# Dense matmuls between the passes of a block inverse, and the order of three groups of loads in the third quarter, in a one-core hybrid RWKV-7 and sparse-attention layer

## The chip, the cores and the metric

The kernel runs on one core of a Trainium2 chip. The metric is the device time of one execution in microseconds (us); less is better. The kernel before takes 1706.21 us, the median of three runs between 1706.05 and 1706.52.

## The reference

One decoder layer in float32 on 1024 tokens of width 1024. A normalized input is projected once by `w_in`. Its parts feed RWKV-7 time mixing (8 heads of 64) and sparse attention, in which an indexer picks 256 keys for each query. Both are projected back, gated channel by channel and merged, and a SwiGLU network follows:

```python
u = rmsnorm(h, norm1_g)
proj = u @ w_in
y_a = rwkv7_mix(token_shift(p_rwkv, tshift_mu), ...)
y_b = dsa_attention(q, k, v, q_idx, k_idx, w_idx)
g_a, g_b = jnp.split(jax.nn.sigmoid(p_gate), 2, axis=-1)
merged = g_a * (y_a @ w_o_rwkv) + g_b * (y_b @ w_o_att)
h = h + merged @ w_out
z_gate, z_up = jnp.split(rmsnorm(h, norm2_g) @ w_ffn_in, 2, axis=-1)
h = h + (jax.nn.silu(z_gate) * z_up) @ w_ffn_out
```

The time mixing is a recurrence over tokens on a state of 64x64 for each head:

```python
sa = einsum('bhij,bhj->bhi', state, -kk_t)
state = state * d_t + sa * (kk_t * a_t) + v_t * k_t
y_t = einsum('bhij,bhj->bhi', state, r_t)
```

To it comes a bonus: the sum of r, k and r_k over a head, times v.

## The kernel before

**Dense work as filling.** The tokens are worked in two halves of 512. Every large product (projections, merge, feed-forward) splits weights and activations into a high and a low part and sums three matmuls of 128x512 for each block of 128 rows (`mm3`, L137: L142 and L143 for the high weights, L147 for the low ones; `mm3_last` with L160 likewise). These products, and attention, are generators in a queue `fill`. `pump(n)` (L177) takes n matmuls' worth from it, and `ticks(n, m)` takes n in m portions. The recurrence calls them between its steps, so dense matmuls fill TensorE while other engines work on a step. TensorE's order is just the order of the calls (it is scheduled by hand); ScalarE (ACT), VectorE (DVE), GpSimd (POOL) and SyncE (SP) get theirs from a scheduler, which places each instruction by its model of when its inputs are there.

**The recurrence.** `rwkv(half, ...)` (L548) runs two quarters of 256 tokens, q = 0 to 3 in all. A quarter's tokens form chunks of 64, each with a triangular system that is solved through the inverses of its two 32x32 blocks. In one quarter, in this order:

- The inputs are loaded, and the sums of the bonus go to memory (`d_bs`, L695). In the third quarter (q = 2) the merge of the first half is put into the queue here (`ready`, `settled`): from then on its products are what fills TensorE.
- Masked products of keys and queries, `MT`, are made by TensorE (L710) and VectorE (L714). Their 32x32 diagonal blocks, the mask blocks, go to memory in eight stores (`d_n`, L721) and come back with matrices along partitions in two loads (`N`, L742).
- VectorE inverts them by forward substitution: 31 steps of two operations (L751 and L753), the first of 128x31, at most of 128x136.
- The inverses go to memory (`d_w`, L755) and come back as blocks (`TT`, L764), which VectorE transposes into `TZ` (L767).
- The bonus sums are loaded, copied over 64 partitions (`bsp`, tile P, L771), and GpSimd multiplies `v` by them (L774).
- `ticks` (L775) then takes dense work from the queue.
- The block inverse: two passes (`pr`), each with 16 tiny 32x32 matmul pairs on `TZ` (L781) and two copies of the result back into `TZ` by ScalarE (L784). Then `inner(0)` (L787, its matmuls L791), a `pump(4)`, tiny matmuls that read those copies (L802), copies into `TT` (L805), and the steps over the chunks (from L843).

**The merge.** `merge(half)` (L1274) makes for each of eight blocks `d` of 128 channels two products in accumulators `acc` of PSUM, of which there are three buffers. `gates(d)` (L1280) loads the two gates into `tmp` tiles (four buffers, shared with attention) through SyncE's queue. VectorE multiplies a product with its gate (L1303, and L1305 or L1309 for the second), adds the two (L1310), ScalarE makes the high part (L1311) and VectorE the low part (L1312). The weights are converted by ScalarE (L116, `whi`) and VectorE (L117, `wlo`), two buffers of each.

`issue_after(x)` is a helper of the scheduler: what is issued inside it stands behind x in the order.

Of the kernel before, what the change touches and what calls it, by code (L numbers as in the profile page):

```python
# [51 lines left out]
def block_kernel(ctx: ExitStack, tc: tile.TileContext, ins: dict, outT: bass.AP, outR: bass.AP, stop=None, dbg=None):  # L52
    nc = tc.nc
    V, A, G, T, SY = nc.vector, nc.scalar, nc.gpsimd, nc.tensor, nc.sync
# [31 lines left out]
    def scratch(name, shape):  # L86
        return [dp.tile(shape, F32, name=f"{name}{h}") for h in range(2)]
# [8 lines left out]
    d_g = scratch("d_g", [16, 128, HT])  # L96
# [4 lines left out]
    d_bs = [dp.tile([2, 4, 256], F32, name=f"d_bs{q}") for q in range(4)]  # L101
    d_n = [dp.tile([64, 32, 32], F32, name=f"d_n{q}") for q in range(4)]
# [3 lines left out]
    def acc():  # L106
        return psA.tile([128, HT], F32, tag="acc", name="acc")

    def mix():
        return psM.tile([128, HT], F32, tag="mix", name="mix")  # L110

    def tmp():
        return tp.tile([128, HT], F32, tag="tmp", name="tmp")
# [63 lines left out]
    def pump(n):  # L177

        credit[0] += n
        while credit[0] > 0 and fill:  # L180
            try:
                credit[0] -= abs(next(fill[0]))
            except StopIteration:
                fill.popleft()
        if not fill:
            credit[0] = 0
# [3 lines left out]
    def ticks(n, m):  # L190

        for i in range(m):
            pump(n * (i + 1) // m - n * i // m)
            next(beside[0], None)
# [331 lines left out]
    def rwkv_consts(p):  # L526
# [18 lines left out]
        p.tile([128, 64], F32, name="edge")  # L545
        return cmask, wup, gup, rmask, ind, ind16

    def rwkv(half, p, consts, ready=None, settled=None):  # L548
        cmask, wup, gup, rmask, ind, ind16 = consts

        def t4(tag, shape=(128, 4, 256)):
            return p.tile(list(shape), F32, tag=tag, name=tag)

        for q in range(2 * half, 2 * half + 2):
# [184 lines left out]

            N = p.tile([128, 32, 32], F32, tag="x6", name="N")  # L740
            for par_ in range(2):
                SY.dma_start(N[64 * par_:64 * par_ + 64], d_n[q])  # L742
            W = p.tile([128, 16, 32], F32, tag="x7", name="W")
            V.memset(W, 0.0)
            for par_ in range(2):
# [22 lines left out]

            bsp = t4("P")
            for e in range(2):  # L770
                SY.dma_start(bsp[64 * e:64 * e + 64].rearrange("p c t -> p (c t)"),  # L771
                             d_bs[q][e].rearrange("c s -> (c s)").partition_broadcast(64))
            bon = v
            G.tensor_tensor(bon, v, bsp, op=ALU.mult)  # L774
            ticks((209, 231, 281, 232)[q], (13, 4, 10, 6)[q])  # L775
            both = [(h, pa, 64 - 64 * pa, 64 * pa) for h in range(8) for pa in range(2)]
            hd = [(h, h // 2, slice((h % 2) * 64, (h % 2) * 64 + 64), slice(h * 64, h * 64 + 64)) for h in range(8)]
            for pr in range(2):
                ps = mix()
                for h, pa, ba, kb in both:  # L780
                    T.matmul(ps[ba + 32:ba + 64, h * 32:(h + 1) * 32], MT[2 * pr + pa][ba:ba + 32, h, ba + 32:ba + 64],  # L781
                             TZ[ba:ba + 32, 0, pr, h, :], start=True, stop=True)
                for ba in (64, 0):
                    A.activation(TZ[ba + 32:ba + 64, 1, pr, :, :],  # L784
                                 ps[ba + 32:ba + 64, 0:256].rearrange("p (h t) -> p h t", h=8), AF.Copy)

            def inner(pr):  # L787
                ps = mix()
# [44 lines left out]
            for pr in range(2):  # L833
                yb = p.tile([128, 2, 512], F32, tag=("P", "x6")[pr], name="yb")
                yc, y2 = yb[:, 0, :], yb[:, 1, :]
                for pa in range(2):
                    c = 2 * pr + pa
# [436 lines left out]
    def merge(half, zp, zs):  # L1274
        yt = yhi, ylo = act_tiles(zp, "y", ("s0", "s1"))
        mt = act_tiles(zp, "m", ("s2", "s3"))
        for j in range(8):
            SY.dma_start(ylo[:, j, :].bitcast(F32), (d_ya if j < 4 else d_yb)[half][j % 4])

        def gates(d):  # L1280
            ga, gb = tmp(), tmp()
            SY.dma_start(ga, d_g[half][d])
            SY.dma_start(gb, d_g[half][8 + d])
            return ga, gb

        first_gates = gates(0) if half == 0 else None
        yield 0
        for j in range(8):
            split(yhi[:, j, :], ylo[:, j, :], ylo[:, j, :].bitcast(F32))
        yield -30  # L1290
        ahead = [weights(ins["w_o"][d]) for d in range(2)] if half == 0 else []
        for d in range(8):
            w = ahead[d] if d < len(ahead) else weights(ins["w_o"][d])
            ga, gb = first_gates if half == d == 0 else gates(d)
            pa = acc()
            pb = None
            if half == d == 0:
                pb = acc()
                yield from mm3_two((pa, pb), w, yt)
            else:  # L1300
                yield from mm3(pa, w, yt, nk=4)
            with tc.high_priority() if pb else nullcontext():
                V.scalar_tensor_tensor(ga, ga, 1.0, pa, op0=ALU.add, op1=ALU.mult)  # L1303
                if pb:
                    V.scalar_tensor_tensor(gb, gb, 1.0, pb, op0=ALU.add, op1=ALU.mult)  # L1305
            if pb is None:
                pb = acc()
                yield from mm3(pb, w, yt, nk=4, wk=4, ak=4)
                V.scalar_tensor_tensor(gb, gb, 1.0, pb, op0=ALU.add, op1=ALU.mult)  # L1309
            V.tensor_tensor(ga, ga, gb, op=ALU.add)  # L1310
            A.activation(mt[0][:, d, :], ga, AF.Copy, scale=0.5)  # L1311
            V.scalar_tensor_tensor(mt[1][:, d, :], ga, 0.5, mt[0][:, d, :].bitcast(F32), op0=ALU.mult,  # L1312
                                   op1=ALU.subtract)
        yield -10
        h = zp.tile([128, 8, HT], F32, tag="s0", name="h")
        load_x(half, h, range(8))
        sq = Rms(h)
        zt = zhi, zlo = act_tiles(zp, "z", ("s1", "s3")) if half == 0 else (None, None)
        pss = []
        if half == 0:  # L1320
            pss = [acc(), acc()]
            yield from mm3_last(pss, [weights(ins["w_out"][d]) for d in range(2)], mt, 8)
        for d in range(8):
            if d < len(pss):
                ps = pss[d]
            else:
                ps = acc()
                yield from mm3(ps, weights(ins["w_out"][d]), mt)
            V.tensor_tensor(h[:, d, :], h[:, d, :], ps, op=ALU.add)
            if half == 0:  # L1330
                A.activation(zhi[:, d, :], h[:, d, :], AF.Copy, scale=par[:, P_N2 + d:P_N2 + d + 1])
            SY.dma_start(d_h[half][d], h[:, d, :])
            sq.add(d)
        if half == 1:
            zs.append(sq)
            return
        for d in range(8):
            V.scalar_tensor_tensor(zlo[:, d, :], h[:, d, :], par[:, P_N2 + d:P_N2 + d + 1],
                                   zhi[:, d, :].bitcast(F32), op0=ALU.mult, op1=ALU.subtract)
        zs.extend((zt, sq))  # L1340
# [548 lines left out]
```

## Time and profile before

| what | us |
|---|---|
| median of three runs | 1706.21 |
| the profiled execution | 1709.14 |
| its span on the core | 1707.2 |
| TensorE busy | 1686.1 (99%) |
| VectorE busy | 1180.9 (69%) |
| ScalarE busy | 896.4 (53%) |
| GpSimd busy | 97.3 (6%) |

The profiled execution is one more run with the recorder on; the lines quoted below are of it, and the times in them are microseconds from the start of the span. In a line of the timeline stand the start, the duration, the engine, the source line, the operation, the tile written and the tiles read, the shapes and the count; a bracket at the end gives the idle time ahead of it on its engine and the instruction that ended it. A window's line gives its length, each engine's busy time, and at the end the granted TensorE clock (1.00 is full speed), the DMA engines' busy share and GB/s.

### The profile page before, as it was taken

To read this page: it belongs to the slowest core of one execution; us is meant where nothing else is said; L and a number is where in the kernel's file an instruction comes from. 1 tells how busy PE (TensorE), PEld (TensorE's weight loads), DVE (VectorE), ACT (ScalarE), POOL (GpSimd) and SP (SyncE) were. 2 spreads that over 40 slices of the span, in tenths; PEclk is the share of its full clock that TensorE was granted. 3 is DMA by queue.
4 is the path that set the end of the run, shared out by engine and by line. 5 is a ranking of instruction groups with operands and counts; after the bars stand their busy time and mean duration, and the time that the engine had idled before them with its cause. 6 is when DMAs were issued, how large, how long until landed. Compare 5 with 4: busy or idle time off the path is not lost.

```text
span 1707.2 us, 28295 instructions
## 1 busy us (share of the span) xinstructions
PE 1686.1 (99%) x10802; PEld 1419.4 (83%) x10802; DVE 1180.9 (69%) x2305; ACT 896.4 (53%) x1727; POOL 97.3 (6%) x107
## 2 busy tenths in 40 slices
PE   9999999999999999999999999999999999999998
PEld 8888888878878777878787888878888899899998
DVE  6789889967567458957886655535564885675764
ACT  6365998453554588755334365533323544353452
POOL 0000000000021110000200110000000000000002
PEclk9999999999999899999999999999999999999999
DMA  6542334436257525653343633244455344524532
GB/s 220 178 136 91 98 104 149 147 108 181 98 177 213 153 95 170 207 171 109 106 123 97 213 128 120 76 154 166 145 185 187 113 156 131 183 95 144 169 113 99
DMA packets 142231, 243.58 MB, mean 143 GB/s; under 512 B 48864, under 2 KB 71072, under 8 KB 141968
## 3 DMA queue, kind: packets, MB, share of 16 engines
q1 hardware_dynamic: 119360, 170.76, 31.3%
q10 hardware_dynamic: 16128, 48.60, 8.5%
q0 software_dynamic: 6608, 22.42, 4.2%
q8 instruction: 85, 1.39, 0.3%
q14 instruction: 50, 0.41, 0.1%
HBM read 188.73 MB, written 53.00 MB: 142 GB/s over the span
## 4 chain that ended last, share of the span: by engine, by line
PE 87%; DVE 5%; DMA 3%; ACT 2%; issue 1%; POOL 1%; SPq 0%; ACTq 0%; POOLq 0%; DVEq 0%
PE acc L142 18%; PE acc L147 18%; PE acc L143 18%; PE acc L160 3%; PE mix L1597 3%; PE mix L1595 3%; PE mix L1594 3%; PE mix L1154 2%; PE mix L958 2%; PE mix L1144 2%; PE mix L1128 1%; PE acc L417 1%; DVE wlo L117 1%; PE mix L142 1%; PE acc L1597 1%
## 5 line engine op out<-in xcount | busy, mean ns | idle before, releaser
L117 DVE TENSOR_TENSOR wlo<-wst,whi 128x1024 fp32r<-128x1024 f32 (+1 forms) x203 | 246.4, 1216 | 181.2 <-PE acc L147 73.9
L116 ACT ACTIVATE whi<-wst 128x1024 fp32r<-128x1024 f32 (+1 forms) x203 | 212.3, 1048 | 185.7 <-PE acc L143 137.1
L142 PE MATMUL acc<-zhi,whi 128*128 128x512 f32 x400 | 158.8, 397 | 0.0
L143 PE MATMUL acc<-zlo,whi 128*128 128x512 f32 x400 | 156.1, 390 | 0.0
L142 PE MATMUL acc<-u1hi,whi 128*128 128x512 f32 x320 | 128.5, 401 | 0.0
L143 PE MATMUL acc<-u1lo,whi 128*128 128x512 f32 x320 | 125.5, 392 | 0.0
L142 PE MATMUL acc<-u0hi,whi 128*128 128x512 f32 (+1 forms) x320 | 122.8, 386 | 0.0
L143 PE MATMUL acc<-u0lo,whi 128*128 128x512 f32 (+1 forms) x320 | 121.3, 382 | 0.0
L147 PE MATMUL acc<-zhi,wlo 128*128 128x512 f32 x400 | 103.1, 395 | 0.0
L142 PE MATMUL acc<-fhi,whi 128*128 128x512 f32 x234 | 91.9, 393 | 0.6 <-ACT whi L116 0.5
L143 PE MATMUL acc<-flo,whi 128*128 128x512 f32 x234 | 91.1, 390 | 0.0
L142 PEld LDWEIGHTS acc<-zhi,whi 128*128 128x128 f32 x400 | 75.1, 188 | 16.9 <-issue 1.8
L143 PEld LDWEIGHTS acc<-zlo,whi 128*128 128x128 f32 x400 | 75.2, 188 | 14.7
L147 PEld LDWEIGHTS acc<-zhi,wlo 128*128 128x128 f32 x400 | 73.6, 188 | 15.6 <-issue 1.2
L147 PE MATMUL acc<-u1hi,wlo 128*128 128x512 f32 x320 | 82.5, 398 | 0.0
L147 PE MATMUL acc<-u0hi,wlo 128*128 128x512 f32 (+1 forms) x320 | 78.7, 384 | 0.0
L1008 ACT ACTIVATE junkl<-kept,z 128x1024 int8<-128x1024 int16 (+1 forms) x64 | 69.4, 1084 | 4.6 <-DVE kept L977 4.4
L142 PEld LDWEIGHTS acc<-u1hi,whi 128*128 128x128 f32 x320 | 60.3, 189 | 12.7 <-issue 0.9
L147 PEld LDWEIGHTS acc<-u1hi,wlo 128*128 128x128 f32 x320 | 59.6, 190 | 12.8 <-issue 0.9
L142 PEld LDWEIGHTS acc<-u0hi,whi 128*128 128x128 f32 x320 | 60.2, 188 | 11.9 <-issue 0.4
L143 PEld LDWEIGHTS acc<-u1lo,whi 128*128 128x128 f32 x320 | 60.5, 189 | 11.3
L143 PEld LDWEIGHTS acc<-u0lo,whi 128*128 128x128 f32 x320 | 60.2, 188 | 11.0
(455 smaller groups left out, 4041.0 us busy)
## 6 DMA issues: line engine op xcount, KB each, us to landing
wst<-in_w_ffn_in SPq DMA_DIRECT2D x72, 512.0 KB, 3.8
wst<-in_w_in ACTq DMA_DIRECT2D x36, 512.0 KB, 3.9
wst<-in_w_in SPq DMA_DIRECT2D x25, 512.0 KB, 4.3
wst<-in_w_fo SPq DMA_DIRECT2D x25, 512.0 KB, 3.5
h<-in_xT SPq DMA_DIRECT2D x32, 256.0 KB, 5.2
d_g<-tmp ACTq DMA_DIRECT2D x32, 256.0 KB, 2.8
k<-d_k POOLq DMA_DIRECT2D x16, 512.0 KB, 5.8
tmp<-d_g SPq DMA_DIRECT2D x32, 256.0 KB, 3.0
```

The costliest lines, as they stand in the source:

```text
L116: A.activation(hi, x, AF.Copy)
L117: V.tensor_tensor(lo, x, hi.bitcast(F32), op=ALU.subtract)
L142: T.matmul(ps, whi[:, wk + k, :], ahi[:, ak + k, tok], start=k == 0, stop=False)
L143: T.matmul(ps, whi[:, wk + k, :], alo[:, ak + k, tok], start=False, stop=False)
L147: T.matmul(ps, wlo[:, wk + k, :], ahi[:, ak + k, tok], start=False, stop=k == nk - 1)
L160: T.matmul(ps, w[:, k, :], a[:, k, tok], start=k == 0 and j == 0, stop=k == nk - 1 and j == 2)
L958: T.matmul(ps[:, :w], iq[:, h, :], ik[:, i, c:c + w], start=i == 0, stop=i == 1)
L1008: A.activation(junka[:, :n], y, AF.Sign, bias=z[:, i:i + 1], accum_out=cnt[:, i:i + 1])
L1144: T.transpose(ps[:, j * 128:(j + 1) * 128], L[:, (c + j) * 128:(c + j + 1) * 128], ident)
L1594: T.matmul(ps, whi[:, k, :], ahi[:, k, :], start=opens and k == 0, stop=False, skip_group_check=True)
L1595: T.matmul(ps, whi[:, k, :], alo[:, k, :], start=False, stop=False, skip_group_check=True)
L1597: T.matmul(ps, wlo[:, k, :], ahi[:, k, :], start=False, stop=k == 3, skip_group_check=True)
```

## The change

Three edits. First, each of the two passes of the block inverse ends with a `pump(4)`, and the `ticks` ahead of them take less: 202 instead of 209 in the first quarter, 223 instead of 231 in the second, 281 as before in the third, 226 instead of 232 in the fourth. Second, in the third quarter the loads of the bonus sums are issued behind those of the mask blocks. Third, in the merge of the first half the gate loads from the second block on are issued behind the mask blocks' second load. Lines from L548 on move down by two to seven in the changed file: L753 becomes L757, L781 L786, L784 L789, L791 L797, L802 L808, L1030 L1036, L1303 L1310.

```diff
--- before.py
+++ after.py
@@ -545,6 +545,8 @@
         p.tile([128, 64], F32, name="edge")
         return cmask, wup, gup, rmask, ind, ind16
 
+    third = []
+
     def rwkv(half, p, consts, ready=None, settled=None):
         cmask, wup, gup, rmask, ind, ind16 = consts
 
@@ -739,7 +741,9 @@
 
             N = p.tile([128, 32, 32], F32, tag="x6", name="N")
             for par_ in range(2):
-                SY.dma_start(N[64 * par_:64 * par_ + 64], d_n[q])
+                asked = SY.dma_start(N[64 * par_:64 * par_ + 64], d_n[q])
+            if q == 2:
+                third.append(asked)
             W = p.tile([128, 16, 32], F32, tag="x7", name="W")
             V.memset(W, 0.0)
             for par_ in range(2):
@@ -768,11 +772,12 @@
 
             bsp = t4("P")
             for e in range(2):
-                SY.dma_start(bsp[64 * e:64 * e + 64].rearrange("p c t -> p (c t)"),
-                             d_bs[q][e].rearrange("c s -> (c s)").partition_broadcast(64))
+                with tc.issue_after(asked.ins) if q == 2 else nullcontext():
+                    SY.dma_start(bsp[64 * e:64 * e + 64].rearrange("p c t -> p (c t)"),
+                                 d_bs[q][e].rearrange("c s -> (c s)").partition_broadcast(64))
             bon = v
             G.tensor_tensor(bon, v, bsp, op=ALU.mult)
-            ticks((209, 231, 281, 232)[q], (13, 4, 10, 6)[q])
+            ticks((202, 223, 281, 226)[q], (13, 4, 10, 6)[q])
             both = [(h, pa, 64 - 64 * pa, 64 * pa) for h in range(8) for pa in range(2)]
             hd = [(h, h // 2, slice((h % 2) * 64, (h % 2) * 64 + 64), slice(h * 64, h * 64 + 64)) for h in range(8)]
             for pr in range(2):
@@ -783,6 +788,7 @@
                 for ba in (64, 0):
                     A.activation(TZ[ba + 32:ba + 64, 1, pr, :, :],
                                  ps[ba + 32:ba + 64, 0:256].rearrange("p (h t) -> p h t", h=8), AF.Copy)
+                pump(4)
 
             def inner(pr):
                 ps = mix()
@@ -1279,8 +1285,9 @@
 
         def gates(d):
             ga, gb = tmp(), tmp()
-            SY.dma_start(ga, d_g[half][d])
-            SY.dma_start(gb, d_g[half][8 + d])
+            with tc.issue_after(third[0].ins) if half == 0 and d else nullcontext():
+                SY.dma_start(ga, d_g[half][d])
+                SY.dma_start(gb, d_g[half][8 + d])
             return ga, gb
 
         first_gates = gates(0) if half == 0 else None
```

TensorE at the block inverse of the third quarter, before (`mhi` and `mlo` are the merged activations, L142 to L147 the dense matmuls that fill):

```order
L142 MATMUL acc<-mhi,whi 128x512
L143 MATMUL acc<-mlo,whi 128x512
L781 MATMUL mix<-TZ,MT 32x32 x32
L791 MATMUL mix<-UV,MT 64x64 x16
L142 MATMUL acc<-mhi,whi 128x512
L143 MATMUL acc<-mlo,whi 128x512
L142 MATMUL acc<-mhi,whi 128x512
L143 MATMUL acc<-mlo,whi 128x512
L802 MATMUL mix<-TT,TZ 32x32 x32
L843 MATMUL mix<-S,AR 128x64 x8
```

and after:

```order
L786 MATMUL mix<-TZ,MT 32x32 x16
L142 MATMUL acc<-mhi,whi 128x512
L143 MATMUL acc<-mlo,whi 128x512
L142 MATMUL acc<-mhi,whi 128x512
L143 MATMUL acc<-mlo,whi 128x512
L786 MATMUL mix<-TZ,MT 32x32 x16
L142 MATMUL acc<-mhi,whi 128x512
L143 MATMUL acc<-mlo,whi 128x512
L142 MATMUL acc<-mhi,whi 128x512
L143 MATMUL acc<-mlo,whi 128x512
L797 MATMUL mix<-UV,MT 64x64 x16
```

The tiny matmuls of the two passes stood together; now they are two groups of 16 with four dense ones behind each. L802, now L808, still follows four dense ones further on.

VectorE where the forward substitution of the third quarter begins (`W`, `tw` and `N` belong to it, `tmp` and `acc` to the merge; the numbers tell buffers' tiles apart), before:

```order
L117 TENSOR_TENSOR wlo_7204<-wst_7201,whi_7203 128x1024
L751 TENSOR_TENSOR tw_6985<-W_6981,N_6978 128x31
L753 TENSOR_TENSOR W_6981<-W_6981,tw_6985 128x31
L1303 SCALAR_TENSOR_TENSOR tmp_7119<-tmp_7119,acc_7123 128x512
L751 TENSOR_TENSOR tw_6985<-W_6981,N_6978 128x30
L1309 SCALAR_TENSOR_TENSOR tmp_7120<-tmp_7120,acc_7137 128x512
L753 TENSOR_TENSOR W_6981<-W_6981,tw_6985 128x30
L1303 SCALAR_TENSOR_TENSOR tmp_7160<-tmp_7160,acc_7164 128x512
```

and after, from the last steps that now stand ahead of the same gate product (`tmp_7119`):

```order
L757 TENSOR_TENSOR W_6981<-W_6981,tw_6985 128x3x26
L755 TENSOR_TENSOR tw_6985<-W_6981,N_6978 128x100
L757 TENSOR_TENSOR W_6981<-W_6981,tw_6985 128x4x25
L755 TENSOR_TENSOR tw_6985<-W_6981,N_6978 128x96
L757 TENSOR_TENSOR W_6981<-W_6981,tw_6985 128x4x24
L1310 SCALAR_TENSOR_TENSOR tmp_7119<-tmp_7119,acc_7123 128x512
L755 TENSOR_TENSOR tw_6985<-W_6981,N_6978 128x115
L1316 SCALAR_TENSOR_TENSOR tmp_7120<-tmp_7120,acc_7137 128x512
L757 TENSOR_TENSOR W_6981<-W_6981,tw_6985 128x5x23
L1317 TENSOR_TENSOR tmp_7119<-tmp_7119,tmp_7120 128x512
```

Ahead of `tmp_7119` stood two operations of the substitution; now it is sixteen, from 128x31 to 4x24, which follow `wlo_7204` as before.

ScalarE ahead of the block inverse of the second quarter (L1030 and L1036 belong to the search for attention's keys, each into a `tmp` tile, L784 and L789 are the copies into `TZ`), before:

```order
L1030 ACTIVATE tmp<-kept_157,top 128x512
L518 DMA d_g_108<-tmp 128x512
L1114 ACTIVATE L,sm<-L,mx 128x256
L1030 ACTIVATE tmp<-kept_157,top 128x512
L1030 ACTIVATE tmp<-kept_156,top 128x512
L1030 ACTIVATE tmp<-kept_156,top 128x384
L784 ACTIVATE TZ<-mix 32x256 x4
```

and after:

```order
L1036 ACTIVATE tmp<-kept_157,top 128x512
L518 DMA d_g_108<-tmp 128x512
L1036 ACTIVATE tmp<-kept_157,top 128x512
L1036 ACTIVATE tmp<-kept_156,top 128x512
L1036 ACTIVATE tmp<-kept_156,top 128x384
L789 ACTIVATE TZ<-mix 32x256 x4
L1120 ACTIVATE L,sm<-L,mx 128x256
```

The four copies still stand behind all of those activations; one softmax step (L1114, now L1120) has gone behind them.

## The prediction

> **What bounds the kernel now.** I read the page first: the busy line of each engine and the chain that ended last.
>
> ```profile
> span 1707.2 us, 28295 instructions
> PE 1686.1 (99%) x10802; PEld 1419.4 (83%) x10802; DVE 1180.9 (69%) x2305; ACT 896.4 (53%) x1727; POOL 97.3 (6%) x107
> PE 87%; DVE 5%; DMA 3%; ACT 2%; issue 1%; POOL 1%; SPq 0%; ACTq 0%; POOLq 0%; DVEq 0%
> ```
>
> TensorE is busy for 1686.1 of 1707.2 us, so 21.1 us is all the idle time there is to win, and the chain runs 87% on it. A change to the order can then do three things only: remove one of TensorE's few waits, add one, or alter the clock at which it works. So the second view is the list of TensorE's waits (total us, times, longest).
>
> ```profile
> PE mix L802 <- ACT TZ L784: 2.7, 3, 2.3
> PE mix L710 <- DVE MT L714: 1.9, 2, 1.1
> ...
> PE mix L781 <- DVE TZ L767: 0.7, 1, 0.7
> ...
> PE acc L142 <- DVE tmp L1303: 0.4, 1, 0.4
> ```
>
> The block inverse (L781 to L802), where the diff puts dense matmuls, waits 2.7 + 0.7 us in all four quarters together, 2.3 of it at one place. The last row, a merge product that waits for a gate product on VectorE, is small now; it matters below.
>
> **Dense matmuls in the block inverse.** Quarters are counted from 0 here; the third is quarter 2. The timeline of TensorE in quarter 0 shows what an alternation of dense and tiny matmuls costs.
>
> ```profile
> 425.96 0.39 PE L142 MATMUL acc<-u0hi,whi 128*128 128x512 f32 x1
> 426.19 0.39 PE L143 MATMUL acc<-u0lo,whi 128*128 128x512 f32 x1
> 426.50 1.20 PE L781 MATMUL mix<-TZ,MT 32*32 32x32 f32 x64
> 428.71 0.50 PE L142 MATMUL acc<-u0hi,whi 128*128 128x512 f32 x1
> 429.05 0.39 PE L143 MATMUL acc<-u0lo,whi 128*128 128x512 f32 x1
> 429.83 1.20 PE L802 MATMUL mix<-TT,TZ 32*32 32x32 f32 x64
> ```
>
> Dense matmuls start 0.23 us apart (425.96, 426.19). The first tiny one after a dense one starts 0.31 behind it, the second dense one after tiny ones 0.34 behind the first: 0.08 + 0.11, about 0.2 us for each pair of changes. L802 bears no wait here and none in the last quarter (the list's three waits are the 2.33, 0.24 and 0.15 us quoted below, in quarters 1 and 2), so the new cover has nothing to hide there. The new order has two more pairs in quarter 0 (+0.4), two more in quarter 2 (+0.4) and one more in quarter 3 (+0.2). In quarter 1 attention's small matmuls, which stood ahead of L781, move between its halves, and the number of matmuls ahead of L802 stays: 0. The dense matmuls themselves are taken from a later place, so their time is no cost. Together **+1.0 us**; the lower bound is 0, if the changes hide behind weight loads.
>
> **The long wait, in quarter 1.** Here are TensorE, then ScalarE, then the windows around it.
>
> ```profile
> 581.21 2.31 PE L802 MATMUL mix<-TT,TZ 32*32 32x32 f32 x64 [2.33 <-ACT TZ L784]
> ...
> 586.37 0.63 PE L142 MATMUL acc<-u1hi,whi 128*128 128x512 f32 x1
> 586.79 0.63 PE L143 MATMUL acc<-u1lo,whi 128*128 128x512 f32 x1
> ```
> ```profile
> 578.91 1.84 ACT L1030 ACTIVATE tmp<-kept,top 128x512 f32<-128x512 int16 x3 [2.26 <-DMA d_yb<-tmp]
> 580.78 1.57 ACT L784 ACTIVATE TZ<-mix 32x256 f32<-32x256 f32 x4
> ```
> ```profile
> 575.00:580.00 5.00, 3.88 (x104) 3.07 (x102) 1.38 (x4) 1.94 (x5) 0.00 (x0) 1.00 0.99 361
> 580.00:582.00 2.00, 0.71 (x16) 0.58 (x18) 1.44 (x3) 1.90 (x6) 0.00 (x0) 0.66 0.14 45
> 588.00:590.00 2.00, 2.00 (x19) 1.75 (x19) 0.43 (x2) 1.92 (x7) 1.20 (x2) 0.50 0.15 39
> 590.00:592.00 2.00, 2.00 (x9) 1.30 (x9) 0.00 (x0) 1.69 (x4) 0.00 (x0) 0.78 0.31 92
> ```
>
> The four TZ copies do not wait for TensorE: they stand on ScalarE behind three L1030 activations, which wait for a `tmp` buffer whose store (d_yb) lands late while the DMA engines are 0.99 busy. In the changed order those activations (now L1036) still stand ahead of all four copies. Splitting L781 makes the first pair's data ready sooner, but ScalarE takes it no sooner, so I leave the wait where it is.
>
> The third number from the end of a window's row, the granted clock, shows what this wait drags along: 0.66 in the first window means half speed from about 580.64 (0.64 x 1 + 1.36 x 0.5 = 1.32), and 0.78 full speed again from about 590.88. The dense matmuls in it start 0.42 apart instead of 0.23, and L802 takes 2.31 instead of 1.20. From 581.21 to 590.88 is 9.7 us of work at half the clock: 4.8 us lost. With the wait the place costs 2.33 + 4.8 = 7.1 us. I take **0** for the change here; the bounds are 0 and -7.1.
>
> **The third quarter: mask blocks first.** On SyncE the bonus sums' two loads now go behind the mask blocks' two; before, they stood ahead. No wait of TensorE's list names either load: the forward substitution starts only when VectorE comes to it. What the new order does change is VectorE's row. Before, two steps of the substitution stand ahead of the second gate product (L1303, now L1310); in the changed kernel sixteen do. Here are ScalarE, VectorE and TensorE there.
>
> ```profile
> 686.15 0.47 ACT L1016 ACTIVATE ge<-cnt,thr 128x1 f32<-128x1 f32 x2
> 686.52 0.47 ACT L1017 ACTIVATE z<-ge,z 128x1 f32<-128x1 f32 x2
> ...
> 688.02 1.04 ACT L116 ACTIVATE whi<-wst 128x1024 fp32r<-128x1024 f32 x1
> ```
> ```profile
> 689.10 1.23 DVE L117 TENSOR_TENSOR wlo<-wst,whi 128x1024 fp32r<-128x1024 f32 x1 [0.98 <-ACT whi L116]
> 690.24 0.18 DVE L751 TENSOR_TENSOR tw<-W,N 128x31 f32<-128x31 f32 x1
> 690.46 0.19 DVE L753 TENSOR_TENSOR W<-W,tw 128x31 f32<-128x31 f32 x1
> 690.57 0.68 DVE L1303 SCALAR_TENSOR_TENSOR tmp<-tmp,acc 128x512 f32<-128x512 f32 x1
> ...
> 699.12 0.26 DVE L753 TENSOR_TENSOR W<-W,tw 128x100 f32<-128x100 f32 x1
> 699.41 0.26 DVE L751 TENSOR_TENSOR tw<-W,N 128x96 f32<-128x96 f32 x1
> ```
> ```profile
> 689.81 1.07 PE L147 MATMUL acc<-yhi,wlo 128*128 128x512 f32 x4
> 691.30 0.50 PE L142 MATMUL acc<-yhi,whi 128*128 128x512 f32 x1 [0.42 <-DVE tmp L1303]
> ```
>
> The accumulator pool has three buffers, so the matmul at 691.30 takes the buffer that L1303 at 690.57 reads: TensorE waits 0.42 us for it now. The sixteen steps stand 0.22 us apart at 128x31 and 0.29 at 128x100: 16 x 0.26 = 4.2 us. They start behind the same wlo, which waits for whi on ScalarE; two small pairs (686.15, 686.52: 0.37 us each, start to start) no longer stand ahead of that, so they may start at 689.4 instead of 690.24. Then L1310 starts between 693.6 and 694.4, ends 0.7 later, and TensorE resumes between 694.3 and 695.1. I take the early end, since VectorE's 0.98 us of idle ahead of wlo shows it free: 694.3 - 691.3 = **+3.0 us** (to +3.8), and the idle stretch grows from 0.42 to about 3.4 us. Queued behind L1310 on VectorE are the rest of the merge's products, each later by as much, but they stay ahead of TensorE, which has three buffers again from there on.
>
> An idle stretch of 3.4 us is longer than the 2.33 us that halved the clock in quarter 1. If it halves it again, dense matmuls follow at once, without the tiny ones that made quarter 1's recovery long; so I take one to two thirds of quarter 1's 10.2 us, 3.4 to 6.8, less up to 1.1 that falls into the wait itself: an estimate of 2.3 to 5.7 us of slow work, half of which is lost, 1.1 to 2.8, middle **+1.9 us**. The Trainium skill, page "TensorE: Matmul & The Clock Gate", sections "Part 1: The HAM clock gate" and "Why this matters for your kernels", asks that idle gaps stay under about 3 us, since one idle window of 3.4 us halves the clock; by that the 2.33 us should have passed, which the trace contradicts. By that rule alone, a gap of 3.4 us would seldom fill a whole window, and the sum would come out without the 1.9.
>
> The substitution itself gets ahead of the merge by fourteen operations, and TensorE comes to L781 later by the stall and the clock, so these waits of the block inverse in quarter 2 should go:
>
> ```profile
> 740.92 0.69 PE L781 MATMUL mix<-TZ,MT 32*32 32x32 f32 x30 [0.73 <-DVE TZ L767]
> ...
> 744.06 0.24 PE L802 MATMUL mix<-TT,TZ 32*32 32x32 f32 x2 [0.24 <-ACT TZ L784]
> 744.46 1.49 PE L802 MATMUL mix<-TT,TZ 32*32 32x32 f32 x62 [0.15 <-ACT TZ L784]
> ```
>
> 0.73 + 0.24 + 0.15 = **-1.1 us**. Next after them comes nothing late in this quarter.
>
> **The sum.** +1.0 (changes of shape) + 0 (quarter 1) + 3.0 (merge wait) + 1.9 (clock) - 1.1 = +4.8 us. The profiled execution took 1709.14 us, 1.94 more than its span, and lies 2.9 above the median of the runs, 1706.21. Against itself it would become 1713.9; at the median's scale I forecast 1711.0 us.
>
> **The rivals.** A measurement of this kernel can tell about 0.2%, 3.4 us, from no change.
>
> *The gap costs no clock* (0.12): TensorE stalls 3.0 us, but the throttle does not act on the gap. For it: the list's wait of 1.1 us at L710 left the clock at full speed. Against it: 2.33 us did not. 1711.0 - 1.9 = 1709.1. The Trainium skill's page "TensorE: Matmul & The Clock Gate" would make this the forecast.
>
> *The stall doesn't come* (0.15): VectorE runs the sixteen steps while TensorE still has matmuls, because the steps start well ahead of 689.4. It decides at a start of 686.4 or sooner, 4.2 + 0.7 us before 691.3. For it: the mask blocks land earlier. Against it: wlo stands ahead and needs whi. Then +1.0 - 1.1 = -0.1: 1706.1. That the mask blocks' place changes nothing, since SyncE's loads were not waited for, gives the same.
>
> *The slow stretch of quarter 1 goes* (0.28), which ends on the other side. The place is 578.9 to 590.9; the price is 4.8 us where only the clock stays up, 7.1 where the wait goes too. It decides where the idle time ahead of 580.64 falls below the 1.8 us that it was (from 581.21 - 2.33 on), or where ScalarE's tmp buffer comes free before 578.9. For it: the point of the drop looks marginal, and work ahead of it shifts by 0.4 us or more. Against it: the order ahead of the copies is the same and the late store is not touched. With the merge stall and its clock (half of this, 0.14): 1711.0 - 7.1 = 1703.9, or 1706.2, no change to tell; without the stall (0.14): 1706.1 - 7.1 = 1699.0, or 1701.3, faster.
>
> *A second slow stretch as long as the first* (0.05): 4.8 lost instead of 1.9: 1713.9.
>
> **How the numbers follow.** The forecast has 0.40. Its own bounds run from 1711.0 - 0.8 - 1.0 = 1709.2 (least clock loss, no cost of shapes) to 1711.0 + 0.8 + 0.9 = 1712.7. Reaching up to 1713.7 leaves out most of the last case, and down to 1701.0 leaves out that part of the faster case that has neither wait nor stall: under 2 in 10 together. Faster by over 3.4 us is the unstalled half of quarter 1's case: 0.14. Slower is the forecast 0.40, the long stretch 0.05, and a third of the 1709.1 case, which lies on the bound: 0.49. The rest, 0.15 + 0.14 + 0.08, is 0.37.
>
> **What would show it.** Right: a wait of about 3.4 us of an L142 merge product for tmp at L1310 in the third quarter, the sixteen steps ahead of it on VectorE, a granted clock of 0.5 in the windows just behind, no wait at the block inverse some 50 us later, and the 2.3 us wait with its slow stretch still in quarter 1. Wrong: the wait at L1310 under 1 us, or the clock at 1.00 in all windows around both places.

## The result, and the profile after

The changed kernel takes 1728.62 us (median of 4 runs, 1727.81 to 1729.95) against 1706.37 of the kernel before in the same comparison: a ratio of 1.0123, 95% interval 1.0108 to 1.0138. It is slower by about 21 us, where 4.8 were forecast. The ratios in this text come with their 95% intervals and can differ a little from the quotient of two medians.

The profiled execution of the changed kernel took 1729.27 us, its span is 1727.2, 20.0 more than before. The head of its page, with the chain (87% on TensorE as before, so the added waits are not one long chain elsewhere):

```profile
PE 1695.0 (98%) x10802; PEld 1423.7 (82%) x10802; DVE 1184.0 (69%) x2305; ACT 899.2 (52%) x1727; POOL 96.4 (6%) x107
...
PE 87%; DVE 6%; ACT 2%; DMA 2%; POOL 1%; issue 1%; SPq 0%; POOLq 0%; DVEq 0%; ACTq 0%
```

The same 10802 matmuls now keep TensorE busy for 1695.0 us instead of 1686.1 (+8.9), and it idles 32.2 us instead of 21.1 (+11.1). TensorE's waits, in us in total, times and the longest:

```profile
PE acc L142 <- DVE tmp L1310: 5.6, 1, 5.6
PE mix L712 <- DVE MT L716: 2.3, 3, 1.4
PE mix L880 <- ACT UV L871: 1.7, 2, 0.9
PE mix L657 <- ACT nrT L651: 1.4, 1, 1.4
...
PE acc L1356 <- ACT yhi L116: 1.3, 1, 1.3
...
PE acc L143 <- DVE zlo L117: 1.2, 1, 1.2
PE mix L868 <- DVE rhs L859: 1.2, 1, 1.2
...
PE mix L808 <- ACT TZ L789: 1.0, 2, 0.8
```

Two things stand here. The merge's wait for its gate product, forecast at 3.4 us, is there with 5.6. And there is a row of waits of 0.7 to 1.4 us that the prediction has no word of: nrT and UV in quarter 1, yhi in quarter 2, MT, UV and rhs in quarter 3, zlo in the last feed-forward part. The block inverse's own waits went from 2.7 + 0.7 to 1.0 us.

Where the clock was halved follows from the granted clock in windows of 1 us. Before: one stretch, from 580.64 to 590.88. After: four, 583.3 to 590.1 (quarter 1), 695.9 to 702.8 (the merge's wait), 849.5 to 856.4 (quarter 3) and 1371.8 to 1375.2 (the last part). One of the new ones, in coarser windows (the third number from the end is the clock):

```profile
848.00:852.00 4.00, 2.84 (x28) 2.55 (x29) 4.00 (x8) 0.63 (x1) 0.00 (x0) 0.69 0.45 133
852.00:856.00 4.00, 4.00 (x23) 3.78 (x21) 1.66 (x3) 1.66 (x3) 0.00 (x0) 0.50 0.61 124
856.00:860.00 4.00, 4.00 (x19) 3.36 (x18) 0.97 (x2) 1.54 (x3) 0.62 (x1) 0.95 0.70 198
```

That gives a ledger: span = work + idle + half of the slow time. Before, 1707.2 - 21.1 - 10.2 / 2 = 1681.0 us of work; after, 1727.2 - 32.2 - 23.9 / 2 = 1683.1. The 20.0 us are 11.1 of idle time, 6.9 of clock and some 2 of work that got longer. Slow time that falls into a wait loses no work: in the changed kernel 2.2 us of it do (695.94 to 698.18), so the clock's share is about 1 us too high there and the work's as much too low. The same sums for the experiments are in a table below.

### The profile page after: what moved, and what is told of

Read it like the earlier page. It is cut to its first block, busy times and chain, and to the rows that moved or that the text cites. A ratio compares the mean times of both kernels' runs of the same rounds, so it can differ in the third digit from the quotient of the medians.

```text
span 1727.2 us, 28294 instructions
## 1 busy us (share of the span) xinstructions
PE 1695.0 (98%) x10802; PEld 1423.7 (82%) x10802; DVE 1184.0 (69%) x2305; ACT 899.2 (52%) x1727; POOL 96.4 (6%) x107
## 4 chain that ended last, share of the span: by engine, by line
PE 87%; DVE 6%; ACT 2%; DMA 2%; POOL 1%; issue 1%; SPq 0%; POOLq 0%; DVEq 0%; ACTq 0%
PE acc L142 19%; PE acc L143 18%; PE acc L147 18%; PE acc L160 4%; PE mix L1601 3%; PE mix L1604 3%; PE mix L1602 3%; PE mix L964 2%; PE mix L1160 2%; PE mix L1150 1%; PE mix L1134 1%; PE acc L417 1%; DVE wlo L117 1%; PE mix L142 1%; PE acc L1604 1%; PE mix L143 1%
## 5 line engine op out<-in xcount | busy, mean ns | idle before, releaser
L142 PE MATMUL acc<-zhi,whi 128*128 128x512 f32 x400 | 159.2, 398 | 0.7 <-ACT zhi L116 0.7
L142 PE MATMUL acc<-u1hi,whi 128*128 128x512 f32 x320 | 128.3, 401 | 0.0
L142 PE MATMUL acc<-u0hi,whi 128*128 128x512 f32 (+1 forms) x320 | 123.0, 387 | 0.0
L147 PE MATMUL acc<-zhi,wlo 128*128 128x512 f32 x400 | 103.7, 399 | 0.0
L142 PE MATMUL acc<-fhi,whi 128*128 128x512 f32 x234 | 92.3, 394 | 0.9 <-ACT whi L116 0.9
L142 PEld LDWEIGHTS acc<-zhi,whi 128*128 128x128 f32 x400 | 75.3, 188 | 18.1 <-issue 2.1
L147 PEld LDWEIGHTS acc<-zhi,wlo 128*128 128x128 f32 x400 | 74.8, 191 | 16.0 <-issue 1.1
L147 PE MATMUL acc<-u1hi,wlo 128*128 128x512 f32 x320 | 82.4, 397 | 0.0
L147 PE MATMUL acc<-u0hi,wlo 128*128 128x512 f32 (+1 forms) x320 | 78.4, 384 | 0.0
L142 PEld LDWEIGHTS acc<-u1hi,whi 128*128 128x128 f32 x320 | 60.4, 189 | 13.0 <-issue 1.3
L142 PEld LDWEIGHTS acc<-u0hi,whi 128*128 128x128 f32 x320 | 60.2, 188 | 11.9 <-issue 0.4
L147 PEld LDWEIGHTS acc<-u1hi,wlo 128*128 128x128 f32 x320 | 59.5, 190 | 12.6 <-issue 0.9
```

The costliest lines, as they stand in the source:

```text
L142: T.matmul(ps, whi[:, wk + k, :], ahi[:, ak + k, tok], start=k == 0, stop=False)
L147: T.matmul(ps, wlo[:, wk + k, :], ahi[:, ak + k, tok], start=False, stop=k == nk - 1)
```

## The experiments

Theory one: two losses that have nothing to do with each other. The load edits put sixteen steps (single operations of the substitution) ahead of the gate product, and the pumps shift the dense filling against the other engines' fixed order. The rival: the late waits follow from the delay in quarter 2.

**Only the pumps** (`pumps_only`): the changed kernel without its two load edits.

```diff
-                with tc.issue_after(asked.ins) if q == 2 else nullcontext():
+                with nullcontext():
-            with tc.issue_after(third[0].ins) if half == 0 and d else nullcontext():
+            with nullcontext():
```

> Only the first edit: the two pump(4) and the smaller ticks; all loads as before. Theory one (two separate losses: the merge's wait in quarter 2, about 9 us, made by the two load edits; and about 10 us in quarter 3 and in the last feed-forward part, made by the pumps, since they shift the dense filling against the other engines' order): five substitution steps instead of two stand ahead of the gate product at L1310, so its wait is about 1.5 us, and the late waits are there: about 1717 (1714 to 1720). Rival (the late waits follow from the delay in quarter 2): 1707 to 1709.

Measured: 1725.92 us, ratio 1.011 (1.0079 to 1.0142). That is nearly the whole loss without the load edits, and above the expected range; the late waits are there, as theory one has it, and cost about twice what it allowed. L808 below is the wait of quarter 1 that the kernel before has too.

```profile
PE mix L712 <- DVE MT L716: 2.7, 3, 1.4
PE mix L808 <- ACT TZ L789: 2.3, 2, 2.1
PE mix L880 <- ACT UV L871: 1.7, 2, 0.9
PE mix L657 <- ACT nrT L651: 1.4, 1, 1.4
```

**Only the loads** (`loads_only`): no pump in the block inverse, ticks of 209, 231, 281, 232, both load edits.

```diff
-            ticks((202, 223, 281, 226)[q], (13, 4, 10, 6)[q])
+            ticks((209, 231, 281, 232)[q], (13, 4, 10, 6)[q])
...
-                pump(4)
```

> Only the two edits to the loads; no pump in the block inverse, ticks as before. Fourteen substitution steps stand ahead of the gate product at L1310. Theory one: its wait is about 5 us, the granted clock drops behind it, 8 to 9 us in all, and quarter 3 and the feed-forward part run as before: about 1715 (1713 to 1717). Rival (the late waits follow from the delay in quarter 2): 1724 to 1728.

Measured: 1713.37 us, ratio 1.0035 (1.0023 to 1.0047), some 6 us. None of the late waits; of the waits that the changed kernel added, the merge's is there alone, and shorter than expected:

```profile
PE acc L142 <- DVE tmp L1309: 3.5, 1, 3.5
PE mix L712 <- DVE MT L716: 1.9, 2, 1.1
```

The clock stayed up behind it, against the expectation, in the profiled execution, which at 1710.12 us was the fastest of seven (1710.12 to 1715.48). The rival falls: a delay in quarter 2 leaves the rest as it was.

**Without the gates' edit** (`no_gates`): pumps, and the bonus sums behind the mask blocks.

```diff
-            with tc.issue_after(third[0].ins) if half == 0 and d else nullcontext():
+            with nullcontext():
```

> The changed kernel without its third edit: pumps, and the bonus sums behind the mask blocks, but the gate loads free. No substitution step stands ahead of the gate product at L1310. Theory one: the 5.6 us wait and the slow clock behind it are gone, the late waits stay: about 1718 (1715 to 1721). Rival (the late waits follow from the delay in quarter 2): 1707 to 1710. If the bonus sums' place alone made the wait, it stays at about 1728.

Measured: 1725.5 us, ratio 1.0112 (1.0095 to 1.0129), above the expected range. The wait for L1310 is gone from TensorE's list, as expected, and the slow clock behind it too. The other waits stand; theory one had set them too low. The wait and the slow work behind it were some 8 us, but the time falls by 2 to 3 only: the profiled execution has two slow stretches that the changed kernel's has not, behind the waits for nrT (510.41 to 513.83) and yhi (681.08 to 684.49). So the losses do not simply add up.

**Only the bonus sums' edit** (`bonus_only`): the kernel before with the second edit.

```diff
-                SY.dma_start(bsp[64 * e:64 * e + 64].rearrange("p c t -> p (c t)"),
-                             d_bs[q][e].rearrange("c s -> (c s)").partition_broadcast(64))
+                with tc.issue_after(asked.ins) if q == 2 else nullcontext():
+                    SY.dma_start(bsp[64 * e:64 * e + 64].rearrange("p c t -> p (c t)"),
+                                 d_bs[q][e].rearrange("c s -> (c s)").partition_broadcast(64))
```

> The kernel before with the second edit alone: the bonus sums' loads behind the mask blocks'. No substitution step stands ahead of the gate product at L1310. Theory: GpSimd's multiply still falls on the first substitution step, which takes some 2 us instead of 0.2, but behind the gate product, so TensorE's wait there is no longer than 0.4 us and the time is that of before, 1705 to 1708. Rival (the bonus sums' place makes the wait by itself): 1712 to 1716.

Measured: 1706.83 us, ratio 0.9996 (0.9983 to 1.0008): no change. The bonus sums' edit puts no step ahead of the gate product; with the gates' edit besides, in `loads_only`, it is fourteen. The gates' edit alone was not run.

**GpSimd's multiply later** (`late_mult`). In the changed kernel the first of the sixteen steps took 2.37 us. VectorE, GpSimd and TensorE there:

```profile
690.05 1.23 DVE L117 TENSOR_TENSOR wlo<-wst,whi 128x1024 fp32r<-128x1024 f32 x1 [1.61 <-ACT whi L116]
691.20 2.37 DVE L755 TENSOR_TENSOR tw<-W,N 128x31 f32<-128x31 f32 x1
...
697.45 0.68 DVE L1310 SCALAR_TENSOR_TENSOR tmp<-tmp,acc 128x512 f32<-128x512 f32 x1
```
```profile
690.30 3.21 POOL L779 TENSOR_TENSOR v<-v,P 128x1024 f32<-128x1024 f32 x1 [32.24 <-DMA P<-d_bs]
```
```profile
698.18 0.79 PE L142 MATMUL acc<-yhi,whi 128*128 128x512 f32 x1 [5.64 <-DVE tmp L1310]
```

In the kernel before the multiply ran earlier, ahead of the substitution:

```profile
683.94 2.50 POOL L774 TENSOR_TENSOR v<-v,P 128x1024 f32<-128x1024 f32 x1 [26.09 <-DMA P<-d_bs]
```

In the changed one it starts while wlo runs and ends at 693.51; the step ends at 693.57. Each seems to wait for the other: the multiply takes 3.21 us here and 2.40 in `bonus_only` (below), the step 2.37 instead of the 0.18 of the kernel before.

```diff
-                V.tensor_tensor(W[:, 0:n, l + 1:32], W[:, 0:n, l + 1:32], o, op=ALU.subtract)
+                stepped = V.tensor_tensor(W[:, 0:n, l + 1:32], W[:, 0:n, l + 1:32], o, op=ALU.subtract)
...
-            G.tensor_tensor(bon, v, bsp, op=ALU.mult)
+            with tc.issue_after(stepped.ins) if q == 2 else nullcontext():
+                G.tensor_tensor(bon, v, bsp, op=ALU.mult)
```

> The changed kernel with GpSimd's multiply of the bonus (L779) issued behind the whole substitution in quarter 2. In the changed kernel the first substitution step takes 2.37 us instead of 0.18 and ends 0.06 us after that multiply does. Theory (VectorE is held while GpSimd's multiply runs): the first step takes 0.2 us, the wait at L1310 falls from 5.6 to about 3.4 us, the time by 2 to 3 us to about 1726. Rival (the first step waits for its mask blocks, or for something else): the step stays long and the time within 1 us of 1728.6.

Measured: 1730.66 us, ratio 1.0139 (1.0124 to 1.0154). The step and the wait did as the theory says:

```profile
694.73 0.18 DVE L755 TENSOR_TENSOR tw<-W,N 128x31 f32<-128x31 f32 x1
```
```profile
699.53 0.50 PE L142 MATMUL acc<-yhi,whi 128*128 128x512 f32 x1 [3.46 <-DVE tmp L1311]
```

5.64 became 3.46, and the difference, 2.18, is what the step lost. But the total did not fall as expected. Its ledger has as much idle time (32.3) and as much slow time (23.9) as the changed kernel's: the wait for yhi is 1.76 instead of 1.34 us and now halves the clock (683.8 to 687.2). The multiply itself moved less than meant: it ran from 691.01 on, beside an idle stretch of VectorE's, since issue order is no wait. In `bonus_only` the same collision hits another instruction:

```profile
686.63 2.40 POOL L779 TENSOR_TENSOR v<-v,P 128x1024 f32<-128x1024 f32 x1 [31.00 <-DMA P<-d_bs]
```
```profile
686.67 2.91 DVE L1316 TENSOR_TENSOR tmp<-tmp 128x512 f32<-128x512 f32 x1
```

L1316 is the merge's sum (L1310 of the kernel before), which took 0.68 us there at 692.69. Here the multiply came first and kept its 2.40 us, and L1316 took 2.2 us longer. The Trainium skill, page "SBUF — State Buffer", section "SBUF: two separate sides", says that VectorE with two SBUF inputs and GpSimd share a port pair, which whoever starts first holds for the whole instruction. These rows agree, both ways round.

**Theory two.** It splits the pumps. What costs is not the alternation of dense and tiny matmuls. It is that 202 + 8, 223 + 8, 281 + 8 and 226 + 8 are 1, 0, 8 and 2 ticks more than before: the queue gives out whole groups of matmuls, so everything that fills behind moves against the recurrence. Two kernels part the two. `equal_fill` has the pumps, and ticks that take exactly as much as before; TensorE's order then differs only inside the block inverses.

```diff
-            ticks((209, 231, 281, 232)[q], (13, 4, 10, 6)[q])
+            ticks((201, 223, 273, 224)[q], (13, 4, 10, 6)[q])
...
+                pump(4)
```

> Loads as before, the two pump(4) in, and ticks reduced to 201, 223, 273 and 224, so that each quarter takes exactly as many dense matmuls from the queue as before: TensorE's order differs from before only inside the block inverses, in 8 rows taken out and 8 put in. Theory two (not the alternation of dense and tiny matmuls costs the 20 us of the pumps, but that 1, 0, 8 and 2 matmuls more are taken in a quarter, which moves everything that fills behind it against the recurrence): none of the late waits, 1706 to 1709, the alternations' 1 us included. Rival (the alternation itself, in the block inverses): 1720 to 1726, with the late waits.

Measured: 1713.95 us, ratio 1.0027 (1.0015 to 1.004), 4 to 5 us by the ratio, above the expected range. No wait at nrT, UV or z; the rest is dearer than expected. The alternations can be read in quarter 0:

```profile
427.08 0.69 PE L786 MATMUL mix<-TZ,MT 32*32 32x32 f32 x32
427.71 0.50 PE L142 MATMUL acc<-u0hi,whi 128*128 128x512 f32 x1
...
433.93 1.11 PE L849 MATMUL mix<-S,AR 64*128 64x64 f32 x16
434.97 0.50 PE L142 MATMUL acc<-u0hi,whi 128*128 128x512 f32 x1
```

From the first tiny matmul to the dense one behind L849 are 7.89 us. Before, they were 5.50, from 426.50 to this row:

```profile
432.00 0.50 PE L142 MATMUL acc<-u0hi,whi 128*128 128x512 f32 x1
```

Eight dense matmuls more are 1.82 of the difference (0.23 each), so two pairs of changes cost 0.57, not 0.4. The wait for TZ at the block inverse of quarter 2, 0.7 us before, has grown, and a slow stretch lies behind it (742.77 to 749.60): with 273 ticks TensorE comes to the first pass eight matmuls sooner.

```profile
PE mix L786 <- DVE TZ L771: 1.6, 2, 1.0
```

`phase_only` is the kernel before with nothing but as many ticks more:

```diff
-            ticks((209, 231, 281, 232)[q], (13, 4, 10, 6)[q])
+            ticks((210, 231, 289, 234)[q], (13, 4, 10, 6)[q])
```

> The kernel before with ticks of 210, 231, 289 and 234 and nothing else: as many matmuls more from the queue in each quarter as the changed kernel takes, no dense matmul inside the block inverse. Theory two: the late waits are there (L655 behind the copy of nrT 1.4 us, L710 1.4, the last feed-forward part's zhi and zlo 0.7 and 1.2), 1718 to 1727. Rival (alternation): 1705 to 1708.

Measured: 1728.46 us, ratio 1.0113 (1.0094 to 1.0132). Eleven ticks, without any pump in the block inverse and without any moved load, cost as much as the whole change, and the late waits of the changed kernel are in the list:

```profile
PE mix L655 <- ACT nrT L649: 2.8, 2, 1.4
PE mix L874 <- ACT UV L865: 2.0, 3, 0.9
...
PE mix L710 <- DVE MT L714: 1.9, 3, 1.4
PE acc L1349 <- ACT yhi L116: 1.6, 1, 1.6
...
PE mix L862 <- DVE rhs L853: 1.2, 1, 1.2
PE acc L143 <- DVE zlo L117: 1.2, 1, 1.2
```

Other waits stand beside them (1.9 us at L802 and 1.2 at L631, both in quarter 2) and the merge's is not among them, so it is partly chance that the two totals agree. Three kernels part the two causes: the pumps with the shift give a ratio of 1.011 (`pumps_only`), the shift alone 1.0113, the pumps alone 1.0027. In the traces TensorE's order behind quarter 0's block inverse first leaves that of the kernel before with the same four dense matmuls, at 439.7 us in the changed kernel and at 441.2 here.

How a shift of four matmuls makes a wait shows at nrT, the first of them. ScalarE before:

```profile
505.16 0.36 ACT L649 ACTIVATE nrT<-mix 16x256 fp32r<-16x256 f32 x1
...
507.87 0.63 ACT L517 ACTIVATE tmp<-tmp 128x512 f32<-128x512 f32 x1 [2.35 <-DVE tmp L516]
```

and in `phase_only`:

```profile
509.93 0.63 ACT L517 ACTIVATE tmp<-tmp 128x512 f32<-128x512 f32 x1 [2.61 <-DVE tmp L516]
510.46 0.36 ACT L649 ACTIVATE nrT<-mix 16x256 fp32r<-16x256 f32 x1
```

The projection that fills ends four matmuls sooner against the recurrence, so its closing activation (L517) now stands ahead of the recurrence's copy and makes it wait 2.61 us for VectorE. That this order is the cause of the wait is read from the rows; it was not tried alone.

**Other shifts.** A few dense matmuls more or fewer in quarter 0 are all that the next four kernels change:

```diff
-            ticks((209, 231, 281, 232)[q], (13, 4, 10, 6)[q])
+            ticks((210, 231, 281, 232)[q], (13, 4, 10, 6)[q])
```

and with 205, 217 and 233 in its place.

> The kernel before with 210 instead of 209 in quarter 0's ticks and nothing else: one more tick makes the queue give out four matmuls more there. Theory two: the waits of quarters 1 and 2 are there (nrT 1.4 us, UV 0.9, S 0.7, yhi 1.3), those of quarter 3 and of the last part need not be, since the other quarters' ticks are as before: 1709 to 1718. Rival (alternation): 1705 to 1708.

> The kernel before with 205 instead of 209 in quarter 0's ticks: four dense matmuls fewer there. Theory two (any shift of the filling against the recurrence and the fixed order of ScalarE and VectorE costs, whichever way): waits of about 1 us at several places behind quarter 0, 1709 to 1720. Rival (what costs is that more matmuls are taken early and are lacking later): 1704 to 1707.

> The kernel before with 217 instead of 209 in quarter 0's ticks: eight dense matmuls more there, a third of a product. Theory two: waits at several places behind quarter 0, other ones than with four; 1708 to 1725. If a phase better than the one chosen exists nearby, it would show as below 1704. Rival (what costs is how many matmuls are taken early): about twice the loss of the shift by four, 1722 to 1730.

> The kernel before with 233 instead of 209 in quarter 0's ticks: 24 dense matmuls more, one whole product of a projection, so that the filling of quarter 1 stands nearly as before against the recurrence (8, 4, 6, 8 matmuls between its steps where 8, 4, 4, 8 stood). Theory two: quarter 1's waits stay those of before, no 1.4 us at nrT, and the time is below that of the shift by four: 1706 to 1715. Rival (what costs is how many matmuls are taken early): more than with four, above 1720.

| quarter 0's ticks | median, us | ratio (interval) |
|---|---|---|
| 205 | 1721.55 | 1.0081 (1.0058 to 1.0103) |
| 210 | 1717.52 | 1.0051 (1.0032 to 1.0071) |
| 217 | 1713.69 | 1.0029 (1.0014 to 1.0043) |
| 233 | 1716.95 | 1.0050 (1.0031 to 1.0069) |

Each is slower than 209, to either side, and the loss does not grow with the number taken: the rival falls. The times of 210 and 217 lie in their expected ranges, those of 205 and 233 a little above. With 233 quarter 1 has no wait at nrT, as expected, but others have come (2.7 us for a projection's tmp at L710 in quarter 2, 2.3 at UV in quarter 3), and that it costs less than 210 is not shown. None was faster than before.

**The whole change with equal filling** (`equal_loads`):

```diff
-            ticks((202, 223, 281, 226)[q], (13, 4, 10, 6)[q])
+            ticks((201, 223, 273, 224)[q], (13, 4, 10, 6)[q])
```

> The whole change, but with ticks of 201, 223, 273 and 224, so that each quarter takes exactly as many dense matmuls from the queue as before. Fifteen substitution steps stand ahead of the gate product at L1310. Theory two: the phase cost goes (none of the waits of nrT, of quarter 3 and of the last part), what stays is about 2 us for alternations and 4 to 8 us for the merge's wait and its clock: 1712 to 1718. Rival (the loads' edits cost only beside shifted filling): 1707 to 1710.

Measured: 1719.28 us, ratio 1.0065 (1.0049 to 1.0082), just above the expected range. The late waits are gone; two waits carry it, each with a slow stretch behind:

```profile
PE acc L142 <- DVE tmp L1310: 5.3, 1, 5.3
PE mix L808 <- ACT TZ L789: 2.9, 2, 2.8
```

The ledger of the profiled executions, in us, slow time added up from windows of 1 us:

| kernel | span | idle | slow time | span - idle - slow / 2 |
|---|---|---|---|---|
| before | 1707.2 | 21.1 | 10.2 | 1681.0 |
| after | 1727.2 | 32.2 | 23.9 | 1683.1 |
| pumps_only | 1725.7 | 29.7 | 23.9 | 1684.1 |
| no_gates | 1722.2 | 27.7 | 20.5 | 1684.3 |
| late_mult | 1728.1 | 32.3 | 23.9 | 1683.9 |
| equal_fill | 1712.6 | 22.5 | 13.7 | 1683.3 |
| equal_loads | 1719.3 | 27.7 | 17.1 | 1683.1 |
| loads_only | 1708.2 | 23.9 | 6.8 | 1680.9 |
| bonus_only | 1704.5 | 21.4 | 3.4 | 1681.4 |
| phase_only | 1728.8 | 33.1 | 27.3 | 1682.1 |

The last column is 1683.1 to 1684.3 with the pumps in the block inverse and 1680.9 to 1682.1 without (1680.8 to 1682.5 in the four kernels of the other shifts): the alternations cost some 2 us. All else is idle time and clock. In `equal_fill` and `phase_only` 3.4 us of the slow time lie in the first 13 us, ahead of everything that the edits touch. The slow time in quarter 1 differs between these executions (10.2, 6.8 or 3.4 us), and so does the wait ahead of it, but the one does not follow from the other: `pumps_only` waits 2.11 us there, the changed kernel 0.85, and both are slow for 6.8.

## Why the prediction was wrong

The direction was right and the size was not: 4.8 us forecast, about 21 measured, outside the range of 1701.0 to 1713.7. By its own steps:

- **"The dense matmuls themselves are taken from a later place, so their time is no cost."** This is the step that failed. It counted matmuls and left out that the ticks do not balance the pumps (1, 0, 8 and 2 ticks more). It gave no reason why what stands behind should keep its time when it comes four matmuls sooner. `phase_only` shows that this imbalance alone gives a ratio of 1.0113. Within the whole change, ticks that balance the pumps bring 1.0123 down to 1.0065 (`equal_loads`): some 10 us of the 21, the largest part of the miss. In the profiled execution of the changed kernel it is the idle time beside the merge's (11.1 - 5.2 = 5.9 us net) and the slow stretches in quarter 3 and the last part (10.2 us, half of it lost). The order on TensorE shows it far behind the block inverse, where the prediction did not look.
- **Changes of shape, +1.0.** The mechanism is right; some 2 us by the ledger for the five pairs, 0.57 for two in quarter 0.
- **The merge's wait, +3.0.** The mechanism is right (`no_gates` and `bonus_only` take it away, `loads_only` has it alone) and mis-sized: from 0.42 to 5.64, +5.2. The term left out is 2.2 us of GpSimd's multiply, which the later loads of the bonus sums moved onto the first of the sixteen steps. The prediction followed the moved loads to their queue and not to the instruction that they release. Without that multiply, in `late_mult`, the wait is 3.46, as forecast; but the steps started at 691.20 instead of 689.4 (689.5 by its own rows), and TensorE came at 692.54 instead of 690.88, and that these two delays cancel is chance.
- **Its clock, +1.9.** Slow from 698.18, where the work resumes, to 702.76: 4.6 us at half speed, 2.3 lost. Right within its bounds, but the reason given does not hold: in `loads_only` a wait of 3.51 us at the same place cost no clock, though it too is longer than 2.33. That tiny matmuls made quarter 1's slow stretch long is not shown either; in `bonus_only` the same ones stand there and it lasts 3.4 us.
- **Quarter 1, 0.** The wait is 0.85 + 0.15 instead of 2.33 us, the slow stretch 6.8 instead of 10.2 us: about 3 us gained, between the bounds. `bonus_only` (0.91 + 0.16 and 3.4) gained more without any pump, and `equal_loads` with pumps has 2.75 and 10.2, so this is not shown to be the change's doing.
- **The waits in quarter 2's block inverse, -1.1.** They went in the changed kernel, and in `loads_only` and `equal_loads` too, as the moved loads would have it. The pumps by themselves do not remove them: `equal_fill` has 1.6 us there.

Of the rivals none came. The stall came with its clock, so neither "the gap costs no clock" nor "the stall doesn't come" holds. The slow stretch in quarter 1 stayed, and the one behind the merge's wait cost 2.3 us, not 4.8. The case that was missing is that filling shifted by a few matmuls costs at some ten places at once. That the direction came out right says little for the forecast, since most of the loss came from a step that it had put at nothing.

## What to carry to other kernels

Where one engine's order is written by hand and the others' is fitted to it, a count that feeds the filling is a phase, not an amount: compare what is taken before and after an edit, and look at the order far behind it. Test such an edit with the counts balanced to the last group, so that it stands alone. And of a load that is moved, follow what it releases, on whichever engine that runs and beside what.

## What the runs showed of the hardware

- **The clock changes on a grid.** In all the profiled executions above each change of the granted clock, once the start is over, lies a multiple of 3.413 us from the others of the same execution until the work ends (in the changed kernel 583.29, 590.12, 695.93, 702.76, 849.53 and on, within 0.02). The Trainium skill, page "TensorE: Matmul & The Clock Gate", section "Part 1: The HAM clock gate", gives a free-running window of 3413 ns, and these agree.
- **A wait's length does not settle whether the clock drops.** `loads_only` waited 3.51 us up to 692.22 and kept full speed; `late_mult` waited 3.46 us up to 699.53 and lost it:

```profile
688.00:692.00 4.00, 0.71 (x4) 0.25 (x2) 3.73 (x12) 2.31 (x6) 0.00 (x0) 1.00 0.46 125
692.00:696.00 4.00, 3.78 (x17) 3.13 (x18) 4.00 (x12) 3.00 (x8) 0.00 (x0) 1.00 0.32 88
```
```profile
696.00:700.00 4.00, 0.54 (x3) 0.43 (x3) 3.66 (x14) 3.90 (x11) 0.00 (x0) 1.00 0.57 190
700.00:704.00 4.00, 4.00 (x13) 3.15 (x12) 2.33 (x8) 1.73 (x4) 0.00 (x0) 0.60 0.23 68
```

  With the grid counted on from the other changes of each execution, the first wait falls into two windows, 1.8 and 1.7 of 3.4 us idle; the second puts 2.1 into one. But idle time within one window does not settle it either. In `no_gates` a wait of 1.53 us at yhi, between matmuls of 128x512, lost the clock (681.08 to 684.49), where the 1.8 us of `loads_only` did not. In `pumps_only` a wait of 1.12 us at L255, with its eight matmuls of two columns behind it in the same window, was enough (800.62 to 804.04). In the changed kernel that wait falls into two windows, and in `late_mult` into one but the eight matmuls nearly all into the next; both kept the clock. The Trainium skill, page "TensorE: Matmul & The Clock Gate", section "Why this matters for your kernels", advises against idle gaps over about 3 us, by which the 1.12 and 1.53 us would have passed. The traces show otherwise.
- **VectorE and GpSimd held each other up.** The multiply of 128x1024 cost the instruction of VectorE that met it, each with two inputs in SBUF, 2.2 us in three kernels: 2.37 instead of 0.18 (the changed kernel), 2.91 instead of 0.68 (`bonus_only`) and 2.43 instead of 0.23 (L755 of 128x78 in `no_gates`). Where VectorE was first, the multiply took 3.21 instead of 2.40. In the kernel before it met a wlo, which took 1.76 instead of 1.23, and which TensorE's list of waits does not name.
